# Shift and scale of the first modulation computed by halves of the channels instead of quarters

## The chip, the cores and the metric

The kernel runs on one core of one Trainium2 chip. The metric is the device time of one execution in microseconds; "before" stands for the kernel as it is, "the change" for the edited one.

## What is computed

One layer of a diffusion backbone on 1024 latent tokens of width 1024 and 256 context tokens. The change touches only the start: the adaLN modulation of the first norm and the projection behind it.

```python
def modulate(h, shift, scale):
    return h * (1 + scale) + shift

def adaln(cvec, w_mod, b_mod):
    return jnp.split(jax.nn.silu(cvec) @ w_mod + b_mod, 6, axis=-1)
...
sh1, sc1, gt1, sh2, sc2, gt2 = [m[:, None] for m in adaln(c, w_mod[l], b_mod[l])]
csh1, csc1, cgt1, csh2, csc2, cgt2 = adaln(c_ctx, w_mod[l], b_mod[l])
...
h = modulate(rmsnorm(x, g_pre1[l]), sh1, sc1)
hc = modulate(rmsnorm(ctx, g_pre1[l]), csh1, csc1)
q, k, v, f, g_a, g_f = split_proj(h @ w_in[l])
```

`w_mod` has 1024 rows of 6 x 1024 columns. Its first 1024 columns give the shift (sh1), the next 1024 the scale (sc1), each for two vectors: c (latent) and c_ctx (context).

## The kernel before, in words

**The projection.** `h @ w_in` is done with a Strassen-Winograd scheme on 2 x 2 blocks: seven products P1 to P7 per pair of output columns. The first half of the channels (0 to 511) and of the tokens (0 to 511) is block B11, the second half of the channels of the same tokens B21. P1 multiplies with B11, P2 with B21, P5 with T1 = (block of the later tokens) - B11. Every operand is split into a high and a low float32r part (`split`, L79 to L81: ACT casts the high part, DVE subtracts to get the low one), and `mm3` (L83 to L87) makes three matmuls of each block of 128 channels. The start of the kernel is an order written out by hand in `tc.manual_schedule()` (from L878): three pairs j = 0, 1, 2 do P1 (`mm(0)` to `mm(2)`), then P2 (`mm(3)` to `mm(5)`), then P5, P6 and P7. `conv(j, p)` splits the weight of one of these products.

**Loads.** All are issued by the SP queue in the order of the program, and each waits until the eighth load ahead of it has landed, so eight of 256 KB are under way at a time. First come tokens 0 to 511 of x (`x_load(0)` to `x_load(3)`, two loads each), then the columns of `w_mod` for shift and scale by quarters of the channels: `wm_stage(q)` issues eight loads (k = 0 to 7, 128 rows each), each with 256 shift columns and 256 scale columns, so rows of 1 KB. Between quarters 1 and 2 stand the three weights A11 of P1; behind quarter 3 stand the later tokens of x (`x_load(4)` to `x_load(7)`) mixed with the weights A12 of P2, then A21 and A22, the rope tables, and `ada_load(g)`: eight loads each for the columns of the later modulation vectors (512 columns wide, rows of 2 KB).

**The modulation by quarters.** `mod_rows(q, ks)` multiplies the staged columns with the two vectors on PE: one matmul of 32 rows per load, four column groups of the array side by side, summed over two rounds. `mod_copy(q)` copies the 128 x 512 result to SBUF (DVE), `mod_turn(q)` sums the four groups and turns the rows into columns with four small matmuls (pm; the trace counts each fp32 matmul of these and of `mod_rows` twice), and `mod_vec(q)` makes from them sx and ax, the shift and scale by channel (six small operations on DVE), for two blocks k of 128 channels.

**What waits for it.** The tokens are normed (`x_square` on ACT, `x_norm` and `x_scale` mostly on DVE) and transposed on PE (`x_turn`, later `turn`). `x_first` applies ax and sx to the transposed tokens straight out of PSUM (ACT for half of the token blocks, DVE for the other), `x_second` does it for the second half of the channels from a copy. `hb_part` splits the result into B11 and B21. Before, quarter 0 is enough for the first half of each P1 product (`mm(j, range(2))`), quarter 1 for its second half, and quarters 2 and 3 likewise for P2. The later tokens (blocks 4 to 7) are normed, scaled and turned between the P2 products, and `t1(c)` (DVE) subtracts to make T1.

Of the kernel before, what the change touches and what calls it, by code (L numbers as in the profile page):

```python
# [40 lines left out]
def block_kernel(ctx: ExitStack, tc: tile.TileContext, t: dict, out: bass.AP, dbg: dict):  # L41
# [413 lines left out]
    nc.vector.tensor_copy(sv32[:, :, 0:2], sv.rearrange("p (c k) -> p k c", c=2))  # L455
    sel = misc.tile([P, 2], F, name="sel")
# [18 lines left out]
    def wm_quarter(a, q, k):  # L475

        load(out=a.rearrange("p (w c) -> p w c", w=2),
             in_=w_mod[k * P:(k + 1) * P, :2 * D].rearrange("p (w c) -> p w c", w=2)[:, :, q * 256:(q + 1) * 256])

    def wm_stage(q):  # L480

        for k in range(KT):
            i = q % 2 * 8 + k
            if i == 15:
                a = misc.tile([P, 512], F, tag="wm", name=f"wm{q}", bufs=6)
            else:
                if i % 3 == 0:
                    st_.append(hbp.tile([P, 3, 512], F, tag="ha", name=f"ws{q}{i}", bufs=10))
                a = st_[-1][:, i % 3, :]
            wms[q, k] = a  # L490
            wm_quarter(a, q, k)
# [73 lines left out]
    sel0 = misc.tile([P, P], F, name="sel0")  # L565
    nc.vector.tensor_scalar_mul(sel0, ones, sel[:, 0:1])

    def mod_rows(q, ks):

        if ks[0] == 0:  # L570
            modp[q] = ps(f"mr{q}")
        for k in ks:
            g = k % 4 * 32
            nc.tensor.matmul(modp[q][g:g + 32, :], sv32[:, k, :], wms[q, k], start=k < 4, stop=k >= 4, skip_group_check=True)

    def mod_copy(q):
        rows = s(f"mc{q}")
        nc.vector.tensor_copy(rows, modp[q])
        modp[q] = rows

    def mod_turn(q):

        pm = ps(f"pm{q}")
        for i in range(4):
            nc.tensor.matmul(pm[:, 2 * i:2 * i + 2], modp[q][:, i * P:(i + 1) * P], sel, start=True, stop=True)
        modp[q] = pm

    def mod_vec(q):
        k0, ks = 2 * q, slice(2 * q, 2 * q + 2)
        for c in range(2):  # L590
            add(sx[:, c, ks], modp[q][:, c:4:2], vec[:, VSH1 + k0:VSH1 + k0 + 2])
            add(ax[:, c, ks], modp[q][:, 4 + c:8:2], vec[:, VSC1 + k0:VSC1 + k0 + 2])
            nc.vector.scalar_tensor_tensor(out=ax[:, c, ks], in0=ax[:, c, ks], scalar=1.0, in1=vec[:, VG1 + k0:VG1 + k0 + 2],
                                           op0=ALU.add, op1=ALU.mult)
# [173 lines left out]


# [108 lines left out]
    with tc.manual_schedule():  # L878
        for tk in range(4):
            x_load(tk)  # L880
        wm_stage(0)
        wm_stage(1)
        for j in range(3):
            pre(j, ("A11",))
        wm_stage(2)
        wm_stage(3)
        x_load(4)
        x_load(5)
        pre(0, ("A12",))
        x_load(6)  # L890
        x_load(7)
        pre(1, ("A12",))
        pre(2, ("A12",))
# [29 lines left out]
        mod_turn(0)  # L923
        mod_vec(0)
# [5 lines left out]
        hb_part(hb, "B11", {c: hraw[c, 0] for c in (0, 2, 1, 3)}, 0, 2)  # L930
        mod_rows(1, range(8))
        ada_load(0, range(KT))
        conv(0, "P1")
        mm(0, range(2))
        mod_copy(1)
        conv(1, "P1")
        mod_turn(1)
        mod_vec(1)
        for tk in range(4):
            x_first(tk, (2, 3), 0, alt_(tk))  # L940
        mm(1, range(2))
        conv(2, "P1")
        hb_part(hb, "B11", {c: hraw[c, 0] for c in (0, 2, 1, 3)}, 2, 4)
        mm(2, range(2))
        mod_rows(2, range(8))
        ada_load(1, range(KT))
        mm(0, range(2, 4))
        mod_copy(2)
# [1170 lines left out]
```

## Time and profile before

| What | Value |
|---|---|
| Time, median of 3 runs | 1377.04 us (1376.99 to 1377.17) |
| Profiled execution: own time, span | 1378.13 us, 1376.3 us |
| PE (matmul) busy | 1288.4 us, 94% of the span |
| DVE busy | 1027.9 us, 75% |
| ACT busy | 687.8 us, 50% |
| POOL busy | 521.4 us, 38% |
| DMA | 219.42 MB, mean 159 GB/s |

The span runs from the first to the last instruction of the program; the execution's own time has some 1.8 us around it. Line numbers are those of the kernel before. A name such as `X_g<-B11a,hP_g` gives the tile written and those read: X and Z are the PSUM sums of P1 and P2, hP and lP the parts of the split weights, mr the result of `mod_rows`, pm that of `mod_turn`, ptx the transposed tokens, hr the modulated ones, ws and wm the staged columns for shift and scale, wa and ar those of the later vectors and their products.

### The profile page before, as it was taken

How to read it: one execution, taken by the hardware profiler on the slowest of the kernel's cores; microseconds unless marked ns; L12 is line 12 of the kernel's file. 1: busy time of each engine (PE TensorE's matmuls, PEld its weight loads, DVE VectorE, ACT ScalarE, POOL GpSimd, SP SyncE). 2: the span in 40 equal slices, each digit the busy share in tenths (PEclk: the TensorE clock that was granted, in tenths of full speed). 3: DMA queues.
4: the chain of work that ended last, by engine and by line, in shares of the span. 5: the costliest groups of instructions: out<-in, count | busy, mean ns of one | idle time of the engine just before them, and what ended most of it. 6: DMA issues, size and time to landing. Idle time of an engine off the chain costs nothing.

```text
span 1376.3 us, 18470 instructions
## 1 busy us (share of the span) xinstructions
PE 1288.4 (94%) x5976; PEld 1029.1 (75%) x5976; DVE 1027.9 (75%) x1713; ACT 687.8 (50%) x1416; POOL 521.4 (38%) x393
## 2 busy tenths in 40 slices
PE   5899999998999999999879999999999988989896
PEld 3457777877878877777657788888888876878674
DVE  4687676787788995735999987666666687796977
ACT  5675334345667764424747554444444444443452
POOL 0000221131334343601584643445444355372754
PEclk9999999999999999999989999999999999999998
DMA  9986273623333435704503554444444569847563
GB/s 307 354 284 191 97 231 117 184 81 116 94 108 109 130 116 182 270 31 130 163 9 98 165 164 130 130 130 127 112 116 114 161 178 287 290 138 226 176 212 123
DMA packets 251125, 219.42 MB, mean 159 GB/s; under 512 B 14972, under 2 KB 204052, under 8 KB 251028
## 3 DMA queue, kind: packets, MB, share of 16 engines
q1 hardware_dynamic: 251028, 218.25, 51.5%
q8 instruction: 47, 0.77, 0.2%
q14 instruction: 50, 0.41, 0.1%
HBM read 159.20 MB, written 58.72 MB: 158 GB/s over the span
## 4 chain that ended last, share of the span: by engine, by line
PE 61%; DVE 18%; DMA 8%; issue 6%; POOL 3%; ACT 3%; SPq 1%; DVEq 0%; POOLq 0%; ACTq 0%
PE X_u L87 5%; PE X_u L86 5%; PE X_u L85 5%; PE Y_u L85 3%; PE Y_u L86 2%; PE Y_u L87 2%; DMA wa<-in_w_mod 2%; DVE p L1277 2%; DVE pl L68 2%; PE X_g L85 2%; PE X_g L87 2%; PE X_g L86 2%; DMA ws<-in_w_mod 2%; PE X_d L85 2%; PE X_d L86 2%
## 5 line engine op out<-in xcount | busy, mean ns | idle before, releaser
L68 DVE TENSOR_TENSOR lP_u<-A_u,hP_u 128x512 fp32r<-128x512 f32 x132 | 103.5, 793 | 45.5 <-ACT hP_u L300 45.5
L362 ACT COPY snP_u<-X_u 128x512 f32<-128x512 f32 x57 | 33.5, 587 | 141.2 <-PE X_u L87 132.7
L68 POOL TENSOR_TENSOR A_u<-A_u,A_u 128x512 f32<-128x512 f32 x44 | 71.5, 1625 | 36.0 <-DVE lP_u L68 18.2
L1297 POOL TENSOR_SCALAR p<-p,sm 128x640 f32<-128x640 f32 (+1 forms) x64 | 48.5, 779 | 84.3 <-PE pp L1302 39.2
L68 POOL TENSOR_TENSOR yd<-yd,snP_d 128x512 f32<-128x512 f32 x36 | 52.2, 1451 | 73.1 <-ACT snP_d L362 73.1
L300 ACT CAST hP_u<-A_u 128x512 fp32r<-128x512 f32 x121 | 74.6, 619 | 0.1
L68 POOL TENSOR_TENSOR A_u<-S_u,A_u 128x512 f32<-128x512 f32 x22 | 29.6, 1344 | 107.5 <-DVE lP_u L68 107.3
L362 ACT COPY snP_d<-X_d 128x512 f32<-128x512 f32 x48 | 28.1, 585 | 83.0 <-PE X_d L87 83.0
L80 ACT CAST ph<-pp 128x512 fp32r<-128x512 f32 x76 | 44.4, 585 | 22.6 <-PE pp L1302 21.3
L68 POOL TENSOR_TENSOR shk<-shk,rope 128x512 f32<-128x512 f32 x2 | 3.2, 1623 | 135.4 <-DMA A_g<-in_w_in 129.6
L68 DVE TENSOR_TENSOR pl<-pp,ph 128x512 fp32r<-128x512 f32 x76 | 51.7, 681 | 3.1 <-ACT ph L80 2.6
L1291 ACT ACTIVATE p<-p,nm 128x640 f32<-128x640 f32 (+1 forms) x64 | 51.3, 802 | 0.7 <-DVE nm L1284 0.7
L68 DVE TENSOR_TENSOR lP_d<-rP_d,hP_d 128x384 fp32r<-128x384 f32 x48 | 43.5, 905 | 10.8 <-ACT hP_d L300 10.5
L1277 DVE CUSTOM_DVE_ANT_0 p<-ss,mask 128x640 f32<-128x640 f32 (+1 forms) x64 | 49.9, 781 | 0.0
L1302 PE MATMUL pp<-ident,p 128*128 128x128 f32 x304 | 46.7, 274 | 3.0 <-POOL p L1297 1.7
L1302 PEld LDWEIGHTS pp<-ident,p 128*128 128x128 f32 x304 | 37.2, 140 | 12.1 <-POOL p L1297 3.2
L68 POOL TENSOR_TENSOR wd<-wd,wd 128x512 f32<-128x512 f32 x22 | 37.5, 1724 | 20.5 <-DVE dB L68 11.5
L1682 DVE SCALAR_TENSOR_TENSOR tb<-u,vec,tb 128x1024 f32<-128x1024 f32 x22 | 39.9, 1814 | 7.2 <-ACT tb L1679 7.2
L1607 POOL TENSOR_SCALAR z<-xr,ry 128x512 f32<-128x512 f32 x15 | 16.7, 1125 | 75.1 <-DVE ry L68 65.0
L68 DVE TENSOR_TENSOR u<-Y_u,snP_u 128x512 f32<-128x512 f32 x22 | 15.2, 690 | 39.8 <-PE Y_u L87 39.8
L68 DVE TENSOR_TENSOR dB<-wd,dB 128x512 fp32r<-128x512 f32 x33 | 38.3, 1171 | 8.5 <-ACT dB L1753 8.4
L68 POOL TENSOR_TENSOR shq<-shq,rope 128x512 f32<-128x512 f32 x8 | 13.1, 1646 | 76.9 <-DMA A_f<-in_w_in 30.0
(894 smaller groups left out, 4658.4 us busy)
## 6 DMA issues: line engine op xcount, KB each, us to landing
A_u<-in_w_up SPq DMA_DIRECT2D x88, 256.0 KB, 3.7
wd<-in_w_down SPq DMA_DIRECT2D x55, 256.0 KB, 4.4
wa<-in_w_mod SPq DMA_DIRECT2D x36, 256.0 KB, 5.4
A_g<-in_w_in SPq DMA_DIRECT2D x32, 256.0 KB, 5.3
ws<-in_w_mod SPq DMA_DIRECT2D x30, 256.0 KB, 6.0
wm<-in_w_mod SPq DMA_DIRECT2D x30, 256.0 KB, 4.5
bP_d<-g_d0P SPq DMA_DIRECT2D x56, 128.0 KB, 3.2
x<-in_x SPq DMA_DIRECT2D x16, 256.0 KB, 5.6
```

The costliest lines, as they stand in the source:

```text
L68: return (eng or nc.vector).tensor_tensor(out=out, in0=a, in1=b, op=op)
L80: copy(hi, src)
L85: nc.tensor.matmul(ps, ah, bh, start=start, stop=False, skip_group_check=True)
L86: nc.tensor.matmul(ps, ah, bl, start=False, stop=False, skip_group_check=True)
L87: nc.tensor.matmul(ps, al, bh, start=False, stop=stop, skip_group_check=True)
L300: copy(st[j]["half", p][0], st[j][STA[p]])
L362: copy(d["s" + p], d["X"])
L1277: nc.vector.tensor_tensor_reduce(out=p_, in0=ssc[:, lo:768], in1=self.mk, op0=ALU.add, op1=ALU.max, scale=1.0, scalar=-3.0e38, accum_out=s ...
L1291: nc.scalar.activation(out=self.pt[g], in_=self.pt[g], func=AF.Exp, scale=SCALE, bias=self.m[:, g:g + 1], accum_out=self.sm[:, g:g + 1])
L1297: nc.gpsimd.tensor_scalar(out=self.pt[g], in0=self.pt[g], scalar1=self.sm[:, g:g + 1], scalar2=1.0, op0=ALU.mult, op1=ALU.mult)
L1302: nc.tensor.transpose(pp[:, g * P:(g + 1) * P], self.pt[g][:, j * P:(j + 1) * P], ident)
L1682: nc.vector.scalar_tensor_tensor(out=tb, in0=u[:, 0:1024], scalar=cw[0], in1=tb, op0=ALU.mult, op1=ALU.add)
```

## The change

- `wm_stage(h)` now works by halves: sixteen loads, k = 0 to 7, shift and scale apart (w = 0, 1), each 512 columns wide, so rows of 2 KB. Bytes and the number of loads stay the same.
- `mod_rows(h)` puts shift and scale of 512 channels into one PSUM bank: two column groups for the shift (even and odd k), two for the scale. The second half's matmuls are placed between the P1 products.
- `mod_copy(h)` copies half of the columns on ACT and half on DVE; `mod_turn` uses a selector of four columns (`sel4`); `mod_vec` makes one vector's values for two blocks k at a time, the context's (c = 1) later than the latent's (c = 0). Two `mod_copy`, two pm tiles and two times four pm matmuls are left of four each.
- P1 begins when the first half is through. The loads are issued as x 0 to 3, first half, A11, second half, A12, x 4 to 7, A21 and A22, rope, `ada_load(0)`, `ada_load(1)`.
- `x_square(4)` and `x_square(5)` stand behind all of B21's splits, and `conv(1, "P2")` ahead of B21's second part; `sel0` is made later in the program.

```diff
--- before.py
+++ after.py
@@ -453,6 +453,8 @@
     nc.vector.tensor_copy(sv32[:, :, 0:2], sv.rearrange("p (c k) -> p k c", c=2))
+    sel4 = misc.tile([P, 2, 2], F, name="sel4")
+    nc.vector.tensor_reduce(out=sel4, in_=ident.rearrange("p (g w c) -> p w c g", g=2, w=2)[:, :, 0:2, :], op=ALU.add, axis=AX.X)
@@ -472,23 +474,18 @@
         for i in range(2):
             load(out=xs[tk][i], in_=x_in[tk * P:(tk + 1) * P, i * 512:(i + 1) * 512])
 
-    def wm_quarter(a, q, k):
-
-        load(out=a.rearrange("p (w c) -> p w c", w=2),
-             in_=w_mod[k * P:(k + 1) * P, :2 * D].rearrange("p (w c) -> p w c", w=2)[:, :, q * 256:(q + 1) * 256])
-
-    def wm_stage(q):
-
-        for k in range(KT):
-            i = q % 2 * 8 + k
+    def wm_stage(h):
+
+        for i in range(2 * KT):
+            k, w = divmod(i, 2)
             if i == 15:
-                a = misc.tile([P, 512], F, tag="wm", name=f"wm{q}", bufs=6)
+                a = misc.tile([P, 512], F, tag="wm", name=f"wm{h}", bufs=6)
             else:
                 if i % 3 == 0:
-                    st_.append(hbp.tile([P, 3, 512], F, tag="ha", name=f"ws{q}{i}", bufs=10))
+                    st_.append(hbp.tile([P, 3, 512], F, tag="ha", name=f"ws{h}{i}", bufs=10))
                 a = st_[-1][:, i % 3, :]
-            wms[q, k] = a
-            wm_quarter(a, q, k)
+            wms[h, k, w] = a
+            load(out=a, in_=w_mod[k * P:(k + 1) * P, w * D + h * 512:w * D + (h + 1) * 512])
 
     st_ = []
 
@@ -562,36 +559,36 @@
 
     modp = {}
 
-    sel0 = misc.tile([P, P], F, name="sel0")
-    nc.vector.tensor_scalar_mul(sel0, ones, sel[:, 0:1])
-
-    def mod_rows(q, ks):
+    def mod_rows(h, ks):
+
 
         if ks[0] == 0:
-            modp[q] = ps(f"mr{q}")
+            modp[h] = ps(f"mr{h}")
         for k in ks:
-            g = k % 4 * 32
-            nc.tensor.matmul(modp[q][g:g + 32, :], sv32[:, k, :], wms[q, k], start=k < 4, stop=k >= 4, skip_group_check=True)
-
-    def mod_copy(q):
-        rows = s(f"mc{q}")
-        nc.vector.tensor_copy(rows, modp[q])
-        modp[q] = rows
-
-    def mod_turn(q):
-
-        pm = ps(f"pm{q}")
-        for i in range(4):
-            nc.tensor.matmul(pm[:, 2 * i:2 * i + 2], modp[q][:, i * P:(i + 1) * P], sel, start=True, stop=True)
-        modp[q] = pm
-
-    def mod_vec(q):
-        k0, ks = 2 * q, slice(2 * q, 2 * q + 2)
-        for c in range(2):
-            add(sx[:, c, ks], modp[q][:, c:4:2], vec[:, VSH1 + k0:VSH1 + k0 + 2])
-            add(ax[:, c, ks], modp[q][:, 4 + c:8:2], vec[:, VSC1 + k0:VSC1 + k0 + 2])
-            nc.vector.scalar_tensor_tensor(out=ax[:, c, ks], in0=ax[:, c, ks], scalar=1.0, in1=vec[:, VG1 + k0:VG1 + k0 + 2],
-                                           op0=ALU.add, op1=ALU.mult)
+            for w in range(2):
+                g = (k % 2 * 2 + w) * 32
+                nc.tensor.matmul(modp[h][g:g + 32, :], sv32[:, k, :], wms[h, k, w], start=k < 2, stop=k >= 6, skip_group_check=True)
+
+    def mod_copy(h):
+        rows = s(f"mc{h}")
+        copy(rows[:, :256], modp[h][:, :256])
+        nc.vector.tensor_copy(rows[:, 256:], modp[h][:, 256:])
+        modp[h] = rows, ps(f"pm{h}")
+
+    def mod_turn(h, js):
+
+        rows, pm = modp[h]
+        for i in js:
+            nc.tensor.matmul(pm[:, 4 * i:4 * i + 4], rows[:, i * P:(i + 1) * P], sel4.rearrange("p w c -> p (w c)"), start=True, stop=True)
+
+    def mod_vec(h, js, c):
+        k0, n = 4 * h + js[0], len(js)
+        ks = slice(k0, k0 + n)
+        pm = modp[h][1][:, 4 * js[0]:4 * (js[0] + n)].rearrange("p (i w c) -> p w c i", w=2, c=2)
+        add(sx[:, c, ks], pm[:, 0, c, :], vec[:, VSH1 + k0:VSH1 + k0 + n])
+        add(ax[:, c, ks], pm[:, 1, c, :], vec[:, VSC1 + k0:VSC1 + k0 + n])
+        nc.vector.scalar_tensor_tensor(out=ax[:, c, ks], in0=ax[:, c, ks], scalar=1.0, in1=vec[:, VG1 + k0:VG1 + k0 + n],
+                                       op0=ALU.add, op1=ALU.mult)
 
 
     w_in = t["w_in"]
...
@@ -879,18 +879,13 @@
         for tk in range(4):
             x_load(tk)
         wm_stage(0)
+        for j in range(3):
+            pre(j, ("A11",))
         wm_stage(1)
         for j in range(3):
-            pre(j, ("A11",))
-        wm_stage(2)
-        wm_stage(3)
-        x_load(4)
-        x_load(5)
-        pre(0, ("A12",))
-        x_load(6)
-        x_load(7)
-        pre(1, ("A12",))
-        pre(2, ("A12",))
+            pre(j, ("A12",))
+        for tk in range(4, 8):
+            x_load(tk)
         for j in range(3):
             pre(j, ("A21", "A22"))
         rope_load()
@@ -920,50 +915,59 @@
         x_raw(3)
         mod_rows(0, range(4, 8))
         mod_copy(0)
-        mod_turn(0)
-        mod_vec(0)
+        ada_load(0, range(KT))
+        ada_load(1, range(KT))
+        mod_turn(0, range(2))
+        mod_turn(0, range(2, 4))
+        mod_vec(0, range(2), 0)
+
         def alt_(i):
             return nc.vector if i % 2 else None
 
         for c in range(4):
             x_first(c, (0, 1), 0, alt_(c))
-        hb_part(hb, "B11", {c: hraw[c, 0] for c in (0, 2, 1, 3)}, 0, 2)
-        mod_rows(1, range(8))
-        ada_load(0, range(KT))
+        b11 = {c: hraw[c, 0] for c in (0, 2, 1, 3)}
+        hb_part(hb, "B11", b11, 0, 2)
         conv(0, "P1")
+        mod_vec(0, range(2, 4), 0)
+        for c in range(4):
+            x_first(c, (2, 3), 0, alt_(c))
+        conv(1, "P1")
+        hb_part(hb, "B11", b11, 2, 4)
+        conv(2, "P1")
         mm(0, range(2))
+        mm(1, range(2))
+        mm(0, range(2, 4))
+        mod_rows(1, range(2))
+        mm(1, range(2, 4))
+        mod_rows(1, range(2, 4))
+        mm(2)
+        for c in range(2):
+            mod_vec(0, range(2 * c, 2 * c + 2), 1)
+        for k in range(4, 8, 2):
+            mod_rows(1, range(k, k + 2))
         mod_copy(1)
-        conv(1, "P1")
-        mod_turn(1)
-        mod_vec(1)
-        for tk in range(4):
-            x_first(tk, (2, 3), 0, alt_(tk))
-        mm(1, range(2))
-        conv(2, "P1")
-        hb_part(hb, "B11", {c: hraw[c, 0] for c in (0, 2, 1, 3)}, 2, 4)
-        mm(2, range(2))
-        mod_rows(2, range(8))
-        ada_load(1, range(KT))
-        mm(0, range(2, 4))
-        mod_copy(2)
-        mod_turn(2)
-        mm(1, range(2, 4))
-        mod_vec(2)
+        ada_load(2, range(KT))
+        mod_turn(1, range(2))
+        mod_turn(1, range(2, 4))
+        mod_vec(1, range(2), 0)
         engs = (nc.vector, None, None, nc.vector)
         b21 = {c: hraw[c, 1] for c in (0, 1, 3, 2)}
         for c in range(4):
             x_second(c, (0, 1), engs[c])
-        mod_rows(3, range(4))
-        mm(2, range(2, 4))
-        mod_rows(3, range(4, 8))
-        ada_load(2, range(KT))
+        mod_vec(1, range(2, 4), 0)
         hb_part(hb, "B21", b21, 0, 2)
         conv(0, "P2")
-        mod_copy(3)
-        mod_turn(3)
+        mm(3, range(2))
+        for c in range(4):
+            x_second(c, (2, 3), engs[c])
+        conv(1, "P2")
+        hb_part(hb, "B21", b21, 2, 4)
+        mm(3, range(2, 4))
         x_square(4)
         x_square(5)
-        mod_vec(3)
+        for c in range(2):
+            mod_vec(1, range(2 * c, 2 * c + 2), 1)
 
         def turn(tk, kh):
             p_ = ps(f"ptx{tk}{kh}")
@@ -974,14 +978,9 @@
         def t1(c, eng=None):
             sub(hraw[c, 0], hraw[c + 4, 0], hraw[c, 0], eng)
 
-        for c in range(4):
-            x_second(c, (2, 3), engs[c])
-        hb_part(hb, "B21", b21, 2, 4)
-        mm(3)
         x_norm(4)
         for tk in (4, 5):
             x_scale(tk, 0, nc.vector)
-        conv(1, "P2")
         x_square(6)
         x_square(7)
         for tk in (4, 5):
```

The order of the instructions moves at three places that the prediction speaks of.

PE, start of P1, before: mr_316 is quarter 0, mr_390 quarter 1, X_g_415 the first P1 sum.

```order
L574 MATMUL mr_316<-ws_154,sv_117 32x512 x2
L574 MATMUL mr_316<-ws_158,sv_117 32x512 x2
L585 MATMUL pm_359<-sel,mc_357 128x2 x4
L574 MATMUL mr_390<-ws_158,sv_117 32x512
L574 MATMUL mr_390<-ws_162,sv_117 32x512 x3
L574 MATMUL mr_390<-ws_166,sv_117 32x512 x3
L574 MATMUL mr_390<-wm_170,sv_117 32x512
L85 MATMUL X_g_415<-B11a_106,hP_g_411 128x512
L86 MATMUL X_g_415<-B11a_107,hP_g_411 128x512
L87 MATMUL X_g_415<-B11a_106,lP_g_412 128x512
```

PE at the same place, the change: mr_318 is the whole first half.

```order
L570 MATMUL mr_318<-ws_160,sv_117 32x512
L570 MATMUL mr_318<-ws_164,sv_117 32x512 x3
L570 MATMUL mr_318<-ws_168,sv_117 32x512 x3
L570 MATMUL mr_318<-wm_172,sv_117 32x512
L582 MATMUL pm_370<-sel_120,mc_367 128x4 x4
L85 MATMUL X_g_461<-B11a_106,hP_g_422 128x512
L86 MATMUL X_g_461<-B11a_107,hP_g_422 128x512
L87 MATMUL X_g_461<-B11a_106,lP_g_423 128x512
L85 MATMUL X_g_461<-B11a_106,hP_g_422 128x512
```

Sixteen loads instead of eight are now multiplied ahead of the pm matmuls, and no mr stands between pm and the first P1 matmul.

PE, inside P1, the change: mr_481 is the second half, X_g_461, X_g_468 and X_g_496 are the P1 sums of pairs 0, 1 and 2.

```order
L87 MATMUL X_g_461<-B11b_108,lP_g_423 128x512
L570 MATMUL mr_481<-ws_180,sv_117 32x512 x3
L570 MATMUL mr_481<-ws_184,sv_117 32x512
L85 MATMUL X_g_468<-B11a_106,hP_g_437 128x512
L86 MATMUL X_g_468<-B11a_107,hP_g_437 128x512
L87 MATMUL X_g_468<-B11a_106,lP_g_438 128x512
L85 MATMUL X_g_468<-B11b_108,hP_g_437 128x512
L86 MATMUL X_g_468<-B11b_109,hP_g_437 128x512
L87 MATMUL X_g_468<-B11b_108,lP_g_438 128x512
L570 MATMUL mr_481<-ws_184,sv_117 32x512 x2
L570 MATMUL mr_481<-ws_188,sv_117 32x512 x2
L85 MATMUL X_g_496<-B11a_106,hP_g_457 128x512
```

The second half's matmuls stand in pieces between the P1 products, the last eight loads of them behind the last P1 product; before, its quarter 2 stood behind the first halves of the P1 products and quarter 3 around the last.

ACT, around the squares of tokens 4 and 5 (junk, x_200 to x_205 before), before:

```order
L80 CAST B21a_238<-hr_349 128x2x128
L80 CAST hP_g_570<-A_g_208 128x512
L500 ACTIVATE junk,ss_581<-x_200 128x512
L500 ACTIVATE junk,ss_581<-x_201 128x512
L500 ACTIVATE junk,ss_581<-x_204 128x512
L500 ACTIVATE junk,ss_581<-x_205 128x512
L540 ACTIVATE hr_327<-hr_327,sx,ax 128x128 x2
L540 ACTIVATE hr_349<-hr_349,sx,ax 128x128 x2
L80 CAST B21a_238<-hr_325 128x128
L80 CAST B21b_240<-hr_325 128x128
```

ACT at the same place, the change (x_208 is the first tile of token block 4):

```order
L80 CAST hP_g_584<-A_g_204 128x512
L80 CAST B21a_240<-hr_331 128x128
L80 CAST B21b_242<-hr_331 128x128
L80 CAST B21a_240<-hr_333 128x128
L80 CAST B21b_242<-hr_333 128x128
L80 CAST B21a_240<-hr_357 128x128
L80 CAST B21b_242<-hr_357 128x128
L80 CAST B21a_240<-hr_355 128x128
L80 CAST B21b_242<-hr_355 128x128
L497 ACTIVATE junk,ss_610<-x_208 128x512
L497 ACTIVATE junk,ss_610<-x_209 128x512
```

The squares stood between the two parts of B21 and now stand behind both, and behind two weight casts hP instead of one.

## Rows read from the trace of the kernel before

**Rows 1.** Windows: length; busy PE, PEld, DVE, ACT, POOL; granted clock; DMA share; GB/s.
```profile
86.50:300.00 213.50, 213.50 (x954) 166.59 (x955) 153.25 (x269) 93.38 (x183) 41.93 (x28) 0.99 0.49 153
...
11.00:12.00 1.00, 0.00 (x0) 0.00 (x0) 0.86 (x5) 0.97 (x4) 0.00 (x0) 1.00 1.10 373
...
46.00:47.00 1.00, 1.00 (x3) 0.81 (x4) 0.93 (x8) 0.96 (x4) 0.00 (x0) 0.50 1.14 278
```

**Rows 2.** The chain that ended last, 0 to 130 us: start, us, what.
```profile
13.33 6.01 DMA ws<-in_w_mod
...
75.29 5.39 DMA wa<-in_w_mod
...
86.50 0.60 PE X_g L86
```

**Rows 3.** Timeline of PE: start, us, engine line op out<-in xcount [idle before <-releaser].
```profile
18.40 1.06 PE L574 MATMUL mr<-ws,sv 128*32 128x512 f32 x8
...
23.16 1.05 PE L574 MATMUL mr<-wm,sv 128*32 128x512 f32 x2
...
25.25 0.50 PE L85 MATMUL X_g<-B11a,hP_g 128*128 128x512 f32 x1 [1.04 <-ACT hP_g L80]
...
36.52 0.48 PE L85 MATMUL X_g<-B11a,hP_g 128*128 128x512 f32 x1
...
38.07 1.06 PE L574 MATMUL mr<-ws,sv 128*32 128x512 f32 x8
...
39.06 0.50 PE L85 MATMUL X_g<-B11a,hP_g 128*128 128x512 f32 x1
...
44.87 1.05 PE L585 MATMUL pm<-sel,mc 128*128 128x2 f32 x8 [3.15 <-DVE mc L578]
...
52.15 1.06 PE L971 MATMUL ptx<-ident,x 128*128 128x128 f32 x8 [0.89 <-DVE x L533]
...
52.97 0.47 PE L85 MATMUL Z_g<-B21a,hP_g 128*128 128x512 f32 x1
...
56.11 2.98 PE L742 MATMUL ar<-wa,sv 128*32 128x512 f32 x8
...
59.02 1.09 PE L971 MATMUL ptx<-ident,x 128*128 128x128 f32 x8
```

**Rows 4.** Timeline of ACT, the same columns.
```profile
21.96 1.51 ACT L540 ACTIVATE hr<-ptx,sx,ax 128x128 f32<-128x128 f32 x4 [2.88 <-DVE ax L593]
...
23.35 1.33 ACT L80 CAST B11a<-hr 128x256 fp32r<-128x256 f32 x4
...
24.56 1.15 ACT L80 CAST hP_g<-A_g 128x512 fp32r<-128x512 f32 x2
...
37.16 1.65 ACT L540 ACTIVATE hr<-hr,sx,ax 128x128 f32<-128x128 f32 x4 [5.10 <-DVE ax L593]
...
38.71 1.31 ACT L80 CAST B21a<-hr 128x256 fp32r<-128x256 f32 x4
...
43.39 0.62 ACT L500 ACTIVATE junk<-x 128x512 f32<-128x512 f32 x1
...
46.41 1.65 ACT L540 ACTIVATE hr<-hr,sx,ax 128x128 f32<-128x128 f32 x4
...
50.29 0.20 ACT L516 ACTIVATE sqx<-vx 128x2 f32<-128x2 f32 x1 [0.65 <-DVE vx L515]
```

**Rows 5.** Timeline of DVE, the same columns.
```profile
7.22 0.18 DVE L68 TENSOR_TENSOR sv<-sv,vec 128x16 f32<-128x16 f32 x1 [4.19 <-ACT warm L445]
...
25.23 0.69 DVE L68 TENSOR_TENSOR lP_g<-A_g,hP_g 128x512 fp32r<-128x512 f32 x1
...
49.91 0.15 DVE L68 TENSOR_TENSOR vx<-ss 128x2 f32<-128x2 f32 x1
...
51.52 0.88 DVE L533 TENSOR_SCALAR x<-x,rx 128x512 f32<-128x512 f32 x2
...
61.44 2.49 DVE L68 TENSOR_TENSOR hr<-hr,hr 128x512 f32<-128x512 f32 x4
```

More of the change, by code (lines that the diff above doesn't have):

```diff
@@ L767, in block_kernel @@
         ada_done(k0 + 13, g)
+    sel0 = misc.tile([P, P], F, name="sel0")
+    nc.vector.tensor_scalar_mul(sel0, ones, sel[:, 0:1])
     hcr, hc, cxt, wkv = {}, {}, {}, {}
```

## The prediction

> **What bounds the kernel now.** I read the windows first. From 86.5 to 300 us PE is busy without a gap [rows 1], and the chain of waits enters PE for good at 86.50 us [rows 2]. So behind 86.5 us PE alone sets the pace for long, and the change, which ends long before, is worth the amount by which it moves that entry. Ahead of it I read the chain and then the timelines of PE, ACT and DVE, to see which wait ends last at each handover. The chain names loads, one behind the other, up to 80.7 us [rows 2]; that is how the SP queue passes from load to load, and it is not by itself proof that an engine waits for them. The timelines show the engines' side: P1 starts at 25.25, the fourth quarter's pm at 44.87 after 3.15 us of idle PE, the later tokens are turned at 52.15 and 59.02 [rows 3], and T1 is begun at 61.44 [rows 5]. From there on ACT and DVE hand the work to each other until 86.5.
>
> **The loads.** With eight loads under way, one lands every eighth of its flight. A load of `w_mod` in 1 KB rows (ws) flies 6.01 us, one in 2 KB rows (wa) 5.39 us [rows 2]: one landing per 0.75 us against 0.67 us, so 0.077 us less for each of the 32. The first half, sixteen loads, is complete 1.2 us earlier than the two quarters were, and everything behind the second half 2.5 us earlier. The Trainium skill, "DMA: Bandwidth & Descriptors", section "Specifications", has it that rows of 512 B or more already run at line rate; by that rule the row length would gain nothing. The two rows above speak against it here. Were it so, the sum below would come out 1.2 us higher, at 1383.1 us.
>
> **P1 starts later.** The last load of the second quarter was multiplied at 23.16 and done 1.05 us later [rows 3]. Less 1.2 us, the first half's rows are done at 23.0. That P1 now needs all sixteen loads is the cost; that x_turn(2) stands behind eight loads instead of four costs nothing, since PE then waits for loads until 21.95 anyway. From the end of quarter 0's rows (18.40 + 1.06) to the first x_first at 21.96 [rows 3, 4] it took 2.5 us: copy, pm, six small DVE operations. Now the copy is two halves, but DVE's waits for ACT's (both read one tile), and three small operations instead of six stand ahead of x_first. No row has a half copy. I bound the stretch by 2.0 and 2.7 us and take 2.3, close to the row. x_first begins at 25.3. From there to the first P1 matmul it was 21.96 to 25.25, 3.29 us [rows 3, 4], so P1 starts at 28.6, **3.35 us late**. Pair 1 needs more: behind hP, DVE makes lP (0.69 us) [rows 5], then three small operations (0.4), then comes x_first for blocks 2 and 3 (1.39, from 21.96 to 23.35) and the next hP (half of 1.15) [rows 4]: 31.6 us.
>
> **PE through P1 and the second half.** From 31.6 PE has work without a gap: three groups of six matmuls at 1.55 us (36.52 to 38.07), sixteen loads at 0.99 us per four (38.07 to 39.06), and twelve matmuls of pair 2 at 3.14 us (52.97 to 56.11) [rows 3]. That is 4.65 + 3.96 + 3.14 = 11.75 us, to 43.35. Here the 3.15 us of idle PE ahead of the last pm are won back: the second half's rows end earlier than pm began before (44.87). Copy, pm and x_second follow 2.3 us later, at 45.65.
>
> **ACT behind it.** This is the place that decides. Before, ACT made B21's first part at 37.16, squared tokens 4 and 5 at 43.39 while it had nothing else, and made the second part at 46.41 [rows 4]. Now everything hangs on one copy, and ACT does it all in a row from 45.65: x_second 1.55 (37.16 to 38.71), four casts 1.21 (23.35 to 24.56), hP 0.57, x_second and eight casts 3.23 (from 46.41 to 0.65 us ahead of 50.29), hP 0.57, four squares 3.02 (43.39 to 46.41) [rows 4]. Together 10.15 us, to 55.8. DVE's norm of tokens 4 and 5 begins there; it began at 49.91 [rows 5]: **5.9 us late**. Norm and scale take 1.61 us to 51.52 [rows 5], and the turn began at 52.15 [rows 3], so it now begins at 58.05. It stands ahead of P2's second product in PE's queue, so that product, whose operands are ready by 53, is queued behind it: 0.82 us later, 58.9, to 62.0. PE is idle for some 3.6 us ahead of the turn.
>
> **What comes back.** Before, PE then spent 56.11 to 59.02, 2.91 us, on four loads of the first ada group, for which 0.99 us is enough; it waited for them. In the change these landed before 57, and 1.9 us are won back. The turn of tokens 6 and 7 begins at 63.0 instead of 59.02 [rows 3]. Their squares (3.02), hP, lP and norm run on ACT and DVE from 56.2 and are through at 62.7 by the same lengths, just hidden. **T1 and all behind it are 4.0 us late**: from 59.02 to 86.50 the order on each engine is the same in both kernels, so I shift it as a whole.
>
> **The clock.** Before, after PE's idle 3.15 us the granted clock fell to 0.50, the 1.2 GHz level [rows 1], for 46 to 49 us and parts of the two neighbours, some 3.2 us, in which matmuls do half their work. The new idle stretch of 3.6 us ahead of the turn is like it. At the start, though, after 8 us without PE work, the clock stayed at 1.00, the 2.4 GHz level [rows 1]. So the price lies between 0 and 1.6 us, half of 3.2. I take **0.9 us**, nearer to the fall, since part of the slow stretch may pass while PE waits. The same fall ahead of P1 or of P2 would be hidden by waits for ACT.
>
> Edits at nothing: `sel4` (one small reduction) and the moved `sel0` stand where DVE idles 4.19 us [rows 5]; without that cover they would cost some 0.5 us. The loads `ada_load(0)` and `(1)` keep their place in SP's queue, behind the rope tables; their buffers are read out before 25 us, and nothing is queued behind a new wait there. The context's `mod_vec` falls on DVE while it waits for the second half. POOL has no part in it.
>
> **The sum.** 4.0 + 0.9 = 4.9 us. The rows come from an execution of 1378.13 us (span 1376.3), 1.1 us above the median of 1377.04; the sum is a difference and I set it on the median: **1381.9 us**. This case's own range: the two copies at 2.0 us each and no fall of the clock give 1380.4; copies at 2.7, a full fall and no gain by longer rows give 1384.6. A difference of 0.2%, 2.75 us, is about what a measurement of this kernel can tell from no change.
>
> **Rivals.**
> 1. *The loads set the pace up to 80 us.* The chain says so up to 80.7 us, and PE did wait for them at 56.11. Then the 2.5 us saved come straight off the end: 1374.5 us. It decides if the turn of tokens 4 and 5 starts by about 52, so that the squares are off the path. Against it: the squares stand behind both parts of B21 on one in-order engine. Chance 0.12.
> 2. *P1 whole is late, but the rest hides it.* PE no longer waits ahead of the second half, and x_second of the second part could then start about when it did (45.65 against 46.41). If ACT and DVE overlap better than my row by row sum, or the stretch up to 86.5 has slack that I don't see, less than 2.75 us is left, about 1378.5. For it: the 3.15 us and 1.9 us that do come back. Against it: 10.15 us of ACT work in a row with no gap for it. Chance 0.18.
> 3. *The longer rows gain nothing.* Both halves then land at the old pace, P1 and the second half's rows come 1.2 us later, and the loads still arrive in time for ar: 1383.1 us, chance 0.05; the two flight times speak against it [rows 2]. It is the rule quoted above.
> 4. *The clock falls more often*, ahead of P1 and inside the second half too, where I have it hidden: up to 1.6 us on top, 1383 to 1383.5, chance 0.10.
>
> The forecast has 0.55. With rivals 3 and 4 it gives slower by over 0.2%, all but 0.02 of theirs: 0.68; within 0.2%: 0.18 and those 0.02, 0.20; faster: 0.12. The range from 1376.5 to 1384.2 leaves out rival 1, and little above.
>
> **What would show it.** Right: sixteen mr loads done near 23; first P1 matmul near 28.6; second half's pm near 44; squares of tokens 4 and 5 ending near 55.8; PE idle over 3 us ahead of the turn at 58; ar of the first group without a wait; T1 begun near 65.5 to 66.5; PE entered for good near 91. Wrong: squares done before 51, a turn at or before 54, or ACT idle between 46 and 55.

## The result and the profile after

The change takes 1382.66 us (median) against 1376.99 us for the kernel before; the ratio is 1.0034, 95% interval 1.0022 to 1.0047, so 4.7 us slower (3.0 to 6.5). One of the seven executions of the change took 1818.36 us at a mean granted clock of 0.655; the median counts it, the ratio does not, and compares the means of the other six and of the seven before (1381.71 and 1377.00 us). A second measurement, below, gave 1.0042 (1.0028 to 1.0056). The profiled execution has a span of 1381.0 us, 4.7 us above that of before. The forecast was 1381.9 us.

The windows of the change, the columns as in [rows 1]:

```profile
25.00:34.00 9.00, 5.05 (x13) 3.47 (x13) 7.66 (x28) 7.35 (x23) 0.00 (x0) 0.62 1.05 388
47.00:64.00 17.00, 11.82 (x30) 8.33 (x31) 12.04 (x51) 14.15 (x44) 0.00 (x0) 0.51 1.01 355
...
85.00:95.00 10.00, 9.33 (x55) 4.74 (x54) 9.93 (x21) 6.48 (x17) 0.00 (x0) 1.00 0.54 175
93.38:300.00 206.62, 206.62 (x931) 161.16 (x932) 152.19 (x265) 90.85 (x177) 41.96 (x28) 1.00 0.50 156
```

PE is entered for good at 93.38 us instead of 86.50 [rows 1]. The granted clock stood at 0.50, the 1.2 GHz level, for nearly all of 47 to 64 us; before, that was some 3 us around 46 to 49 [rows 1]. It was also at 0.50 from 27 to 33 us, inside P1, where it stood at 1.00 before.

The chain of waits of the change, as [rows 2]. The flight of a load for shift and scale fell from 6.01 to 5.42 us, near the 5.39 of a load with 2 KB rows in the kernel before [rows 2]:

```profile
13.62 5.42 DMA ws<-in_w_mod
...
93.38 0.50 PE X_g L86
```

The timeline of PE in the change, as [rows 3]:

```profile
22.45 1.04 PE L570 MATMUL mr<-wm,sv 128*32 128x512 f32 x2
...
28.80 0.79 PE L85 MATMUL X_g<-B11a,hP_g 128*128 128x512 f32 x1 [3.77 <-ACT hP_g L80]
...
44.67 1.07 PE L582 MATMUL pm<-sel,mc 128*128 128x4 f32 x8 [0.57 <-ACT mc L574]
49.66 0.79 PE L85 MATMUL Z_g<-B21a,hP_g 128*128 128x512 f32 x1 [3.92 <-ACT hP_g L80]
...
58.35 1.97 PE L975 MATMUL ptx<-ident,x 128*128 128x128 f32 x8 [1.99 <-DVE x L530]
59.98 0.78 PE L85 MATMUL Z_g<-B21a,hP_g 128*128 128x512 f32 x1
...
64.92 1.07 PE L739 MATMUL ar<-wa,sv 128*32 128x512 f32 x8
65.91 1.10 PE L975 MATMUL ptx<-ident,x 128*128 128x128 f32 x8
...
78.32 0.63 PE L85 MATMUL Y_g<-T1a,hP_g 128*128 128x512 f32 x1
...
93.38 0.50 PE L86 MATMUL X_g<-T2a,hP_g 128*128 128x512 f32 x1 [0.67 <-DVE T2a L68]
...
96.12 1.07 PE L739 MATMUL ar<-wa,sv 128*32 128x512 f32 x8
```

The timeline of ACT, as [rows 4], from the copy of the second half on:

```profile
44.25 0.37 ACT L574 COPY mc<-mr 128x256 f32<-128x256 f32 x1 [10.29 <-PE mr L570]
46.23 1.65 ACT L537 ACTIVATE hr<-hr,sx,ax 128x128 f32<-128x128 f32 x4 [1.61 <-DVE ax L590]
...
52.97 0.29 ACT L80 CAST B21b<-hr 128x128 fp32r<-128x128 f32 x1
53.17 0.63 ACT L497 ACTIVATE junk<-x 128x512 f32<-128x512 f32 x1
```

The timeline of DVE, as [rows 5], with the norm of tokens 4 and 5 and the start of T1:

```profile
56.19 0.16 DVE L68 TENSOR_TENSOR vx<-ss 128x2 f32<-128x2 f32 x1 [1.52 <-ACT junk L497]
...
68.33 2.49 DVE L68 TENSOR_TENSOR hr<-hr,hr 128x512 f32<-128x512 f32 x4
```

ACT idles 10.29 us for the second half's rows, and then everything comes at once: from 46.23 us x_second, the casts of B21, two weights, and only from 53.17 the squares of tokens 4 and 5. Their norm (vx) begins at 56.19 instead of 49.91 [rows 5], the turn at 58.35 instead of 52.15, T1 at 68.33 instead of 61.44 [rows 3, 5].

One interval helps to read all the runs. I call "entry" the first ar behind the product that begins at T2a (96.12 us here). T2 is the next operand made from T1, on ACT and DVE. In the kernel before the entry was at 90.80 us. The timeline of PE before, from that product on:

```profile
85.17 0.50 PE L85 MATMUL X_g<-T2a,hP_g 128*128 128x512 f32 x1 [1.10 <-ACT T2a L80]
86.50 0.60 PE L86 MATMUL X_g<-T2a,hP_g 128*128 128x512 f32 x1 [0.83 <-DVE T2a L68]
86.89 0.63 PE L87 MATMUL X_g<-T2a,lP_g 128*128 128x512 f32 x1
...
90.80 1.06 PE L742 MATMUL ar<-wa,sv 128*32 128x512 f32 x8
```

From T1 to entry took 29.36 us before, and 27.79 in the change. From T1 to the second matmul at T2a, which waits for DVE, it is 25.05 us in both (61.44 to 86.50, 68.33 to 93.38); what differs is PE's product behind it, 4.30 us before, most of it at a granted clock of 0.50, and 2.74 us at 1.00 in the change. In the change the clock was at 0.50 in the first product with T1 instead (78 to 81 us), PE came later to T2a, and its 1.10 us of idle time ahead of that product are gone. Span less entry is 1285.5 and 1284.9 us. So T1 came 6.9 us later, the entry 5.3, the end 4.7.

### The profile page after: what moved, and what is told of

Read it like the earlier page. It is cut to its first block, busy times and chain, and to the rows that moved or that the text cites. A ratio compares the mean times of both kernels' runs of the same rounds, so it can differ in the third digit from the quotient of the medians.

```text
span 1381.0 us, 18440 instructions
## 1 busy us (share of the span) xinstructions
PE 1290.1 (93%) x5960; PEld 1029.4 (75%) x5960; DVE 1027.1 (74%) x1712; ACT 687.0 (50%) x1418; POOL 520.0 (38%) x393
## 4 chain that ended last, share of the span: by engine, by line
PE 62%; DVE 17%; DMA 8%; issue 5%; ACT 3%; POOL 3%; SPq 1%; DVEq 0%; POOLq 0%; ACTq 0%
PE X_u L86 5%; PE X_u L87 5%; PE X_u L85 5%; PE Y_u L85 2%; PE Y_u L87 2%; PE Y_u L86 2%; PE X_d L85 2%; DVE pl L68 2%; DVE p L1276 2%; PE X_d L86 2%; PE X_d L87 2%; PE X_g L85 2%; PE X_g L86 2%; PE X_g L87 2%; DMA wm<-in_w_mod 1%
```

## The experiments

Ratios are to the kernel before, run on the same chips; 0.2% is 2.75 us.

**1. Only the place of the squares, in the kernel before.** `x_square(4)` and `x_square(5)` go behind `hb_part(hb, "B21", b21, 2, 4)`.

```diff
-        x_square(4)
-        x_square(5)
         mod_vec(3)
...
         hb_part(hb, "B21", b21, 2, 4)
+        x_square(4)
+        x_square(5)
         mm(3)
```

> The kernel before, with only the four squares of tokens 4 and 5 moved behind both parts of B21 on ACT, as the change has them. Theory: the norm begins near 52.7 us instead of 49.91, the turn near 54.9 instead of 52.15; 1.9 us come back since PE need not wait for the loads of ar, so the turn of tokens 6 and 7 is 0.9 us late, and up to 1.5 us more by the clock after PE's new idle 3.7 us: 1377.9 to 1379.5 us. Rival (that P1 waits for the whole half is the whole loss, the place of the squares nothing): 1377.0 us, T1 at 61.4.

Ratio 1.0023 (1.0012 to 1.0035), 1379.57 us. The timeline of PE, the turn of tokens 4 and 5 and the first ar:

```profile
55.59 1.90 PE L969 MATMUL ptx<-ident,x 128*128 128x128 f32 x8 [3.56 <-DVE x L533]
...
60.98 1.07 PE L742 MATMUL ar<-wa,sv 128*32 128x512 f32 x8
```

The timeline of DVE, norm and T1:

```profile
53.33 0.16 DVE L68 TENSOR_TENSOR vx<-ss 128x2 f32<-128x2 f32 x1 [2.58 <-ACT junk L500]
...
64.39 2.49 DVE L68 TENSOR_TENSOR hr<-hr,hr 128x512 f32<-128x512 f32 x4
```

The norm waits for ACT's squares, the turn is 3.4 us late and runs at the slow clock, the wait of ar is won back, T1 is 2.95 us late (0.8 us of it from the last pm, which was that much late in this execution, with the clock at 0.50 from 28 to 35 us). The order of P1 is that of the kernel before. The move of the squares alone costs 3.2 us of time (1.7 to 4.8); the rival falls.

**2. The squares in ACT's idle stretch, in the change.**

```diff
+        x_square(4)
+        x_square(5)
         mod_copy(1)
```

and the two lines behind B21 go.

> The change, with only the four squares of tokens 4 and 5 moved on ACT to ahead of the copy of the second half, where ACT idles 10.29 us in the changed kernel. Theory (ACT's work in a row behind that copy sets the turn of tokens 4 and 5): the row on ACT from x_second to the last cast of B21 is 6.9 us instead of 9.9, the norm of tokens 4 and 5 begins when DVE comes to it, near 54.7 us instead of 56.19, the turn near 56.9 instead of 58.35, T1 1.5 us sooner, and up to 2.7 us more if the clock comes back before the second P2 product: 1381.2 down to 1378.5 us. Rival (loads or other work behind 60 us set the pace): turn sooner, T1 and the time as in the change, 1382.7 us.

Ratio 1.0024 (1.0013 to 1.0034), 1379.2 us. The timeline of DVE, the start of T1:

```profile
64.56 2.49 DVE L68 TENSOR_TENSOR hr<-hr,hr 128x512 f32<-128x512 f32 x4
```

vx began at 54.11, the turn at 56.27, T1 at 64.56 us, 3.8 us sooner than in the change, of which 0.5 stand already at the first half's pm; the clock came back between 56 and 57 us instead of 64. At the turn 1.6 us are gained beyond those 0.5, at T1 3.3; the rest between the two is the clock. The stretches are those of the theory; in the time the intervals of this kernel and of the change overlap.

**3. The second half's rows ahead of P1's last product.**

```diff
         mm(1, range(2, 4))
         mod_rows(1, range(2, 4))
-        mm(2)
...
         mod_copy(1)
+        mm(2, range(2))
...
         mod_turn(1, range(2, 4))
+        mm(2, range(2, 4))
```

> The change, with the last eight matmuls of the second half's rows ahead of the P1 product of pair 2 on PE instead of behind it, and its two parts around the pm matmuls. Theory (the second half's copy is late because its rows stand behind P1 in PE's order, not because of its loads, of which the last landed at 36.2 us): the copy near 41.2 instead of 44.25 us, pm near 42.6 instead of 44.67, x_second and the row on ACT behind it 2.1 us sooner, T1 and the time 2 us below the change, 1380.6 us. Rival (the loads hold the second half up): copy, x_second and time as in the change, 1382.7 us.

Ratio 1.0008 (1.0000 to 1.0017), 1378.07 us, better than expected; the interval lies clear of that of the change. The timeline of PE, the second half's pm:

```profile
41.95 0.95 PE L582 MATMUL pm<-sel,mc 128*128 128x4 f32 x8
```

The timeline of DVE, the start of T1:

```profile
63.80 2.49 DVE L68 TENSOR_TENSOR hr<-hr,hr 128x512 f32<-128x512 f32 x4
```

pm began at 41.95 us, vx at 53.35 and T1 at 63.80, 4.5 us sooner than in the change, of which 0.7 stand already at the first half's pm (23.22 against 23.96). Some 2 us are the sooner copy; the rest is the clock, at 1.00 again from 54 us. The loads did not hold the second half; PE's order did.

**4. Are loads the bound? The rope tables moved.**

```diff
-        rope_load()
...
         ada_load(1, range(KT))
+        rope_load()
```

> The change, with the four loads of the rope tables behind the sixteen loads for ar instead of ahead of them, so that those land 2.7 us sooner. Rival of the prediction (loads set the pace up to 80 us): T1 sooner, up to 2.7 us less, 1380 us. Theory (from the turn of tokens 4 and 5 on nothing waits for a load in the change): no difference, 1382.7 us, T1 at 68.3.

Ratio 1.0036 (1.0024 to 1.0048), T1 at 68.44 us: nothing. Rival 1 of the prediction falls for the change.

**5. Rows of 1 KB in the change.** Each load fetches 256 shift and 256 scale columns; `mod_vec` picks the values accordingly.

```diff
-            load(out=a, in_=w_mod[k * P:(k + 1) * P, w * D + h * 512:w * D + (h + 1) * 512])
+            load(out=a.rearrange("p (w c) -> p w c", w=2),
+                 in_=w_mod[k * P:(k + 1) * P, :2 * D].rearrange("p (w c) -> p w c", w=2)[:, :, (2 * h + w) * 256:(2 * h + w + 1) * 256])
```

> The change, with the sixteen loads of a half as 256 shift and 256 scale columns each, so rows of 1 KB as before; bytes, number and order of the loads stay. Theory (a landing per 0.75 us with 1 KB rows against 0.67): the first half complete about 1.2 us later than in the change, P1 at 30.0 instead of 28.80, all behind it up to the turn of tokens 4 and 5 as much later, 1383.9 us. Rival (rows of 512 B or more already go at line rate, so the row length gains nothing): P1 at 28.8, 1382.7 us.

Ratio 1.0054 (1.0039 to 1.0068); this interval overlaps that of the change. The timeline of PE, the start of P1:

```profile
30.01 0.80 PE L85 MATMUL X_g<-B11a,hP_g 128*128 128x512 f32 x1 [3.78 <-ACT hP_g L80]
```

P1 began at 30.01 us (28.80 in the change, 29.13 in its second profile below, and between 28.07 and 29.03 in the other runs made from it), T1 at 69.69, 1.4 us later. This pair, and 6.01 against 5.42 us of flight, say that 2 KB rows still gain about a tenth over 1 KB here. Rival 3 falls. The Trainium skill, "DMA: Bandwidth & Descriptors", section "Specifications", puts line rate at rows of 512 B and more. The two flights do not agree with that.

**6. Rows of 2 KB in the kernel before.**

```diff
-        load(out=a.rearrange("p (w c) -> p w c", w=2),
-             in_=w_mod[k * P:(k + 1) * P, :2 * D].rearrange("p (w c) -> p w c", w=2)[:, :, q * 256:(q + 1) * 256])
+        load(out=a, in_=w_mod[k * P:(k + 1) * P, q * 512:(q + 1) * 512])
```

> The kernel before, with each of the 32 loads for shift and scale fetching 512 columns side by side (rows of 2 KB) instead of 256 and 256; which columns a load brings is then not the one the kernel needs, so shift and scale have other values, and nothing else differs. Theory (0.077 us less per load, 2.5 us in all, and before the kernel waits for these loads at P1, at the last quarter and at ar): P1 1.2 us sooner at its second quarter, T1 2 to 2.5 us sooner, 1374.5 to 1375 us. Rival (row length gains nothing, or what waits for loads before is hidden): 1377.0 us.

Ratio 0.9995 (0.9987 to 1.0004): a miss. The last pm began at 44.77 us (44.87 before), vx at 49.80 (49.91). It does not follow that this stretch waited for no load before. The timeline of ACT before, the first weight cast of P2, and behind it that of DVE here, the copy of quarter 3:

```profile
42.87 0.62 ACT L80 CAST hP_g<-A_g 128x512 fp32r<-128x512 f32 x1 [2.85 <-DMA A_g<-in_w_in]
```

```profile
44.02 0.69 DVE L577 COPY mc<-mr 128x512 f32<-128x512 f32 x1 [0.62 <-PE mr L573]
```

Before, ACT waited 2.85 us for the load of this weight, DVE's lP waited for ACT, and the copy stood behind lP. With sooner loads that wait is gone. But in this execution the granted clock was 0.50 from 27 to 33 us, where it stood at 1.00 before; PE came to quarter 2's rows at 34.49 instead of 32.37 us, and the copy of quarter 3 now waited for PE. The wait of ar went too, and T1 came at 60.76, 0.7 us sooner. So in this execution one wait took the place of another; what the sooner loads are worth in the kernel before without this fall of the clock stays open. In the change they count once, at P1.

**7. The clock held up.** Matmuls on constants, overwritten afterwards, fill PE's idle time in the change: 7 ahead of P1, 8 ahead of P2, 4 ahead of the turn.

```diff
+    def warm(dst, n):
+        for _ in range(n):
+            nc.tensor.matmul(dst[:, :256], ident, filler[0], start=True, stop=True, skip_group_check=True)
```

> The change, with idle PE filled by matmuls whose result is overwritten: 7 ahead of P1, 8 ahead of the first P2 product, 4 ahead of the turn of tokens 4 and 5, some 0.43 us each. If they keep the granted clock at 1.00 from 26 to 64 us: P1's matmuls up to 33.7 us, the turn (0.9 us) and the second P2 product (1.8 us) are not slowed, T1 2.7 to 3.5 us sooner, 1379.2 to 1380 us. Rival (the clock costs the 0.9 us of the prediction, the rest is hidden): 1381.8 us. If PE's slower matmuls cost nothing: 1382.7 us.

Ratio 1.0027 (1.0013 to 1.0041), 1381.05 us. The windows:

```profile
25.00:34.00 9.00, 7.17 (x28) 4.52 (x27) 7.75 (x27) 7.36 (x23) 0.00 (x0) 1.00 1.05 384
47.00:64.00 17.00, 12.75 (x60) 8.24 (x58) 12.06 (x48) 14.29 (x45) 0.00 (x0) 1.00 1.06 389
```

The timeline of PE, from the turn of tokens 4 and 5 to that of 6 and 7:

```profile
57.77 1.12 PE L991 MATMUL ptx<-ident,x 128*128 128x128 f32 x8 [1.34 <-DVE x L539]
...
61.60 1.07 PE L753 MATMUL ar<-wa,sv 128*32 128x512 f32 x8
62.59 0.66 PE L991 MATMUL ptx<-ident,x 128*128 128x128 f32 x4
64.08 0.66 PE L991 MATMUL ptx<-ident,x 128*128 128x128 f32 x4 [0.83 <-DVE hr L548]
```

The clock stayed at 1.00 through both windows. From the turn to ar took 3.83 us instead of 6.57, 2.7 us less; but now PE waits 0.83 us for DVE, and T1 came at 66.05, 2.3 us sooner than in the change, 1.9 when the 0.4 us by which this execution's first pm was sooner are taken off. The last pm (44.06 against 44.67) moved by 0.2 us beyond that: the slow clock in P1 was hidden, as predicted. The 1.9 us lie between the 2.7 to 3.5 that were expected and the rival's 0.9; in the time the intervals of this kernel and of the change overlap, so the price is read from the profiles alone.

**8. The change once more.**

> The change once more, as it is, beside the kernel before. Theory (the stretches read in its first profile are those of the kernel, not of one execution): P1 at 28.4 to 29.1, turn of tokens 4 and 5 at 58 to 58.6 at a clock of 0.50, T1 at 68.0 to 68.5, PE entered for good at 93.1 to 93.6, 0.3 to 0.4% above the kernel before. Rival (the fall of the clock, or where it falls, differs from execution to execution): T1 up to 2.7 us sooner, or the clock down near 94 us.

Ratio 1.0042 (1.0028 to 1.0056). The rival is partly right. The timeline of PE in this execution, the turn and the P2 product behind it:

```profile
58.96 1.97 PE L975 MATMUL ptx<-ident,x 128*128 128x128 f32 x8 [2.01 <-DVE x L530]
...
64.06 1.07 PE L739 MATMUL ar<-wa,sv 128*32 128x512 f32 x8
65.05 1.09 PE L975 MATMUL ptx<-ident,x 128*128 128x128 f32 x8
```

and further on, the product at T2a and the entry:

```profile
91.22 0.51 PE L85 MATMUL X_g<-T2a,hP_g 128*128 128x512 f32 x1 [1.08 <-ACT T2a L80]
92.55 0.80 PE L86 MATMUL X_g<-T2a,hP_g 128*128 128x512 f32 x1 [0.82 <-DVE T2a L68]
93.14 0.63 PE L87 MATMUL X_g<-T2a,lP_g 128*128 128x512 f32 x1
...
96.80 1.07 PE L739 MATMUL ar<-wa,sv 128*32 128x512 f32 x8
```

The clock came back at 61.6 us instead of 64, and T1 began at 67.47. But now PE idled 1.08 and 0.82 us at T2a, the clock fell there, and T1 to entry took 29.33 us, as in the kernel before. In the first product with T1 (76.51 to 79.39 us) the clock stood at 1.00 this time. The entry (96.80) is no sooner than in the first profile (96.12).

**9. Is that fall what the kernel before pays?** A first try put three such filler matmuls ahead of the product at T2a, in the bank of the next ar:

> The kernel before, with three matmuls whose result is overwritten (some 0.43 us each) in PE's idle 1.10 us ahead of the product that begins at 85.17 us, behind which the granted clock fell to 0.50 for 86.9 to 90 us. Theory (the kernel before pays 1.4 to 1.6 us there that the change does not, since in the change PE waits less at this place and keeps the clock): the clock holds, the next ar begins near 89.4 instead of 90.80 us, 1375.4 us. Rival (the two kernels do not differ there, what the change wins back lies elsewhere): the clock falls as before or its fall costs nothing, 1376.9 us.

Ratio 1.0013 (1.0003 to 1.0023), no answer: the bank was not free, PE waited 2.37 us for ACT's copy out of it, and the clock fell all the same. The second try makes ar's first four matmuls twice:

```diff
-        for k in range(half * 4, half * 4 + 4):
+        for k in list(range(half * 4, half * 4 + 4)) * (2 if (g, half) == (3, 0) else 1):
```

> The kernel before, with the first four matmuls of the fourth ar group made twice (the second time overwrites the first), so that PE works 1 us longer just ahead of the product that begins at 85.17 us, in the stretch in which it idled 1.10 us. Theory (that idle time lets the clock fall to 0.50 for 86.9 to 90 us, and the kernel before pays 1.57 us for it): PE idles only some 0.7 to 0.9 us there, the clock stays at 1.00, the ar behind the product begins 27.8 us after T1 instead of 29.36, and the time is 1375.4 us. Rival (the fall does not hang on this idle time, or its loss is made up later): 29.4 us after T1, 1377 us.

Ratio 0.9989 (0.9980 to 0.9997), 1375.11 us. T1 began at 62.36, and PE did not idle at T2a and went through that product at a clock of 1.00. Its timeline, in the first product with T1 and at T2a:

```profile
72.40 0.63 PE L87 MATMUL Y_g<-T1a,lP_g 128*128 128x512 f32 x1
...
87.09 0.50 PE L85 MATMUL X_g<-T2a,hP_g 128*128 128x512 f32 x1
87.43 0.49 PE L86 MATMUL X_g<-T2a,hP_g 128*128 128x512 f32 x1
87.76 0.40 PE L87 MATMUL X_g<-T2a,lP_g 128*128 128x512 f32 x1
...
90.17 1.07 PE L742 MATMUL ar<-wa,sv 128*32 128x512 f32 x8
```

27.81 us from T1 to entry, with 1 us of useless work on PE, and 1.5 us less time (0.4 to 2.8): the price is there to be won. This profile does not show that the repeated matmuls won it, though, for here the clock fell in the first product with T1 (71 to 74 us), as in the first profile of the change, and that alone makes PE late for T2a. In run 6, which has the order of the kernel before and no repeated matmuls, the clock fell there too (71 to 74 us), and it took 27.79 us. All thirteen profiles fit this. Nine have the clock at 0.50 in the first product with T1 and at 1.00 at T2a, and take 27.77 to 27.81 us from T1 to entry; four (before, run 1, run 8 and the first try here) have it the other way round, and take 29.33 to 29.37 us, or 30.86 with the wait for the bank.

**10. A version from the theory.** The halves with 2 KB rows stay, and P1 still begins with the whole first half. x 4 to 7 are loaded ahead of A12; the second half's rows stand ahead of the last P1 products; the squares of tokens 4 to 6 fill ACT's idle stretch; the norm of tokens 4 and 5 stands just ahead of B21's first part, their scale and turn between its two parts; the turn of tokens 6 and 7 stands ahead of ar; the rope tables are loaded behind the loads for ar. The core of it:

```diff
+        x_square(4)
         mm(0, range(2))
         mm(1, range(2))
         mm(0, range(2, 4))
+        mod_rows(1, range(8))
...
         mod_copy(1)
+        x_square(5)
+        x_square(6)
+        mm(1, range(2, 4))
...
+        mm(2)
...
+        x_norm(4)
         hb_part(hb, "B21", b21, 0, 2)
```

> A version built from the theory: the halves with 2 KB rows, x 4 to 7 loaded ahead of A12, the second half's rows ahead of the last P1 products, the squares of tokens 4, 5 and 6 in ACT's idle stretch, norm, scale and turn of tokens 4 and 5 between the parts of B21, the turn of tokens 6 and 7 ahead of ar, the rope tables behind the loads for ar. Theory: x_second near 43 us, T1 near 58 instead of 68.3 (before 61.4); if nothing new waits 3 us below the kernel before, 1373.5 us. Rival (the loads for ar, of which the sixteenth lands near 63, then set the pace as they did in the kernel before): T1 is sooner, PE waits for ar's loads behind it, and the time is 1375 to 1377 us.

Ratio 0.9972 (0.9961 to 0.9983), 1373.12 us: faster than both. The timeline of ACT, the last square and x_second:

```profile
42.05 0.64 ACT L497 ACTIVATE junk<-x 128x512 f32<-128x512 f32 x1
...
42.68 1.64 ACT L537 ACTIVATE hr<-hr,sx,ax 128x128 f32<-128x128 f32 x4
44.23 0.19 ACT L513 ACTIVATE sqx<-vx 128x2 f32<-128x2 f32 x1
```

The timeline of DVE, the start of T1:

```profile
58.70 2.49 DVE L68 TENSOR_TENSOR hr<-hr,hr 128x512 f32<-128x512 f32 x4
```

x_second follows the squares without a gap, and the square root for the norm of tokens 4 and 5 runs right behind its first part. T1 began at 58.70 us and ar did not wait for loads. P1 began at 28.87 us, as in the change: a late P1 can be made up. Which of the moves gives how much, this run does not tell.

## Why the prediction was right, point by point

- **Right in sign, size and main mechanism.** The prediction named ACT's in-order row as the place that decides. First half's rows done at 23.5 us (23.0 predicted), P1 28.80 (28.6), pair 1 31.90 (31.6), x_second 46.23 (45.65), ACT's row 9.9 us (10.15), vx 56.19 (55.8), turn 58.35 (58.05). Runs 1 to 3 show that the row sets T1: beyond what stood already at a pm, the move alone costs 2.1 us there, a shorter row gives 3.3 back, a sooner one 3.8 (1.7 us of each of these two is the clock that came back sooner). The second weight cast that now stands ahead of the squares, 0.5 us of the row, was not tried by itself.
- **What comes back.** ar ran 1.07 us without a wait instead of 2.98 [rows 3]: the 1.9 us predicted.
- **The clock was mis-sized.** The step was "I take 0.9 us", between 0 and 1.6. From start to start the turn took 1.63 us instead of 0.82, the P2 product behind it 4.94 instead of 3.14 [rows 3]: 2.6 us more. The forecast had a fall of some 3 us behind the idle time ahead of the turn. The clock fell sooner, at 47 us, after PE had idled 3.92 us ahead of P2's first product, and stayed at 0.50 until 64 us, through the turn and the whole product behind it; PE's idle time ahead of the turn was 1.99 us and not over 3. Run 7 puts the price at T1 at 1.9 us, after DVE's own pace takes 0.8 back. Rival 4 came true in half: the clock did fall inside P1 as well, but run 7 finds only 0.2 us of that at the last pm.
- **"I shift it as a whole" was wrong by 1.6 us the other way.** From 59.02 to 86.50 the order is the same, but the kernel before has a price in it that need not be carried along: PE idle ahead of T2a, then a slow product. In the first profile of the change a slow product with T1 came first, PE arrived later and did not idle, so 27.79 instead of 29.36 us. Run 8 shows that the change pays the price in another execution, run 6 that the order of the kernel before does not always pay it. So the 1.6 us hang on the execution; whether they come more often in the one kernel than in the other, so few profiles cannot say.
- **The sum.** 6.2 (turn) + 2.6 - 1.9 = 6.9 at T1, - 1.6 = 5.3 at the entry, 4.7 at the end. The two misses cancel, so 4.9 was right for a reason that is only partly its own, and partly by luck: T1 and the entry of PE, which were to come near 66 and 91 us, came at 68.33 and 93.38. In the second profile the balance is another: T1 6.0, the entry 6.0 and the span 5.6 us above before. The last 0.6 us lie within what span less entry varies from run to run (1283.8 to 1285.6 us among these profiles) and stay unexplained. Nor is one profile of before exact to better than a microsecond: T1 began at 61.44 us there, at 62.39 and 62.36 in the two kernels of run 9, which are the same program up to that point.
- **Rivals.** The loads (1) fell with the turn at 58.35 us and with run 4; run 6 adds that sooner loads did not shorten the kernel before, though not why. The longer rows gaining nothing (3) fell with run 5. That the rest hides it (2) fell with the result.
- **Slips that change nothing in the sum.** The fall before was 3.4 us long by its windows (0.89 at 45 to 46 us, 0.50 for three, 0.90 at 49 to 50), not 3.2. The 21.95 us stands in no row; the last load of quarter 1 was multiplied at 23.16 [rows 3]. Rival 1's 1374.5 us is 2.5 us below before, so within 0.2%, and was counted as faster.

## What to carry to other kernels

When work is batched (two quarters into one half), look at which engine sat idle during the wait and what it then has to do in a row: the loss was not the later first product but the row of work behind one late copy, with four squares in it that no longer had an idle slot in an in-order queue. Fill the new wait with the work whose inputs are already there, before judging the batching; here that turned 4.7 us lost into 3.8 us won. A gain in transfers counts only at the handovers where the transfer lands last, and only until the next wait takes over, as in run 6.

## What the runs showed of the hardware

- The clock moves its price around. In two executions of the change it came back at 64 and at 61.6 us; the second reached T1 0.9 us sooner and paid 1.5 us at 92 us. A fall in the first product with T1 made that product 1.6 us longer (4.47 us in the first profile, 2.88 in the second) and cost nothing at T2a, 25.05 and 25.08 us behind T1; a fall at T2a made the product there as much longer, and it all came out at the entry. The Trainium skill, "TensorE: Matmul & The Clock Gate", section "Part 1: The HAM clock gate", says that one kernel shows different numbers of slow matmuls at its start from run to run. These two profiles show the like, some 60 and 90 us behind the start.
- Filler on PE is no free cure: it held the clock at 1.00 from 25 to 64 us and removed 2.7 us of slow matmuls, but 1.9 us arrived at T1; in the other kernel, without a free bank, it became a wait of 2.37 us. The kernel with four matmuls repeated in a bank that was held anyway was 1.5 us faster (0.4 to 2.8).
